# A list scheduler inside a kernel: operands that are also the result are counted, other durations in its cost table

## Chip, cores, metric

One core of a Trainium2 chip runs the whole program. The metric is the device time of one execution in microseconds; lower is better. Five engines have queues of their own: TensorE (PE, with its weight loads PEld), VectorE (DVE), ScalarE (ACT), GpSimd (POOL) and SyncE (SP), which issues the DMAs.

## What is computed

Two layers of a hybrid backbone on 640 tokens: 512 latent ones that are denoised and 128 context tokens, in float32, width 1024. Cut to what matters:

```python
def layer(x, cond):
    shift, scale, gate = split(silu(cond) @ w_mod + b_mod)
    h = rms_norm(x) * (1 + scale) + shift
    cols = split_cols(h @ w_in)             # q, k, v, gates for four mixers
    y = [neighbourhood_attention(cols), hgrn2(cols), mla(cols), window_attention(cols)]
    y = [o * silu(z) for o, z in zip(y, cols.z)]
    merged = sum(sigmoid(cols.g[b]) * (y[b] @ w_branch[b]) for b in range(4))
    return x + gate * (merged @ w_out)
x = layer(layer(x)); y = rms_norm(x)        # plus new keys, values and states as outputs
```

`hgrn2` is a gated linear recurrence in both directions, computed by chunks of 64 tokens; the decay between two tokens comes from the exponential of a difference of cumulated logarithms.

## The kernel before

All activations are held with features on the partitions and the 640 tokens along the free axis, in two halves of 320 columns. Each float32 matrix product is three matmuls of rounded parts: high times high, high times low, low times high. So each weight tile `wraw` (128x1024) is loaded by SyncE and split by two operations into `whi` (a copy) and `wlo` (a subtraction), and a projection half is 24 matmuls of 128x320 into a PSUM tile `pj_<name>`. Projections named `hq`, `hf`, `hb`, `ho`, `hz` belong to the recurrence, `ckv` and `qa` to latent attention (`mla`), `n..` to neighbourhood attention, `w..` to window attention, `g<branch><d>` to the merge gates; `pjm` is the product with `w_branch`, `pjo` that with `w_out`. Most working tiles have the name `slot`.

`hg_mix` is the recurrence. For each of eight levels it forms two tiles K and Q of decays (differences, then Exp, then products with keys and queries) and multiplies them on TensorE in 20 small products into `pslev`; VectorE or ScalarE copies these into place. Before that come Sigmoid and Ln on ScalarE, after it norms with Sqrt. Each change among these sets of functions is a table load on ScalarE. In the level loop, `K0, K1 = vw(K)` are views, and the products with the keys are

```python
                self.tt(K0, K0, kf0, ALU.mult)
                self.tt(K1, K1, kb1, ALU.mult)
```

so that the first input is the same object as the result. The attention parts (`probs`, `attend`, `pv_pair`) compute scores into `psS`, reduce them on VectorE into a column `nm`, take Exp on ScalarE, scale by the reciprocal `rc` of the sum, transpose on TensorE into `psT`, split, and multiply with the values into `psO`.

Nothing of this is issued as it is written. Every call is recorded as an operation by `Recorder.add`, with its predecessors; operations that may run on more than one engine are recorded with alternatives by `Recorder.alts` (`tt`, `ts`, `cpy`, `half`). `make_call` gives each alternative an engine time `step`, a time to the result `lat` and a flag `lock`. Then `Recorder.order` plays the program through in planned time: each engine that becomes free takes the ready operation of the lowest priority number; `take` gives an operation with alternatives to the engine that would end it first; an operation with `lock` waits until the last one with `lock` has ended, on VectorE or GpSimd; a table load costs 1290 ns more; TensorE's operations count double for a while after a long idle time. Slots and PSUM tiles are handed out as they come free in planned time. `emit` then issues each engine's operations in that order, and all instructions carry the line of `emit` (L561). `PLAN` is a hand-written interleaving of projections and mixing steps, `RANK` shifts whole kinds of steps, `AHEAD` and `WAHEAD` set how far the order may run ahead; the change touches none of them.

Of the kernel before, what the change touches and what calls it, by code (L numbers as in the profile page):

```python
# [22 lines left out]
P = 128  # L23
# [24 lines left out]
def f32(ap):  # L48
# [3 lines left out]

CAPS = {"slot": NSLOT, "w": NW, "ps": 8, "col": 32, "hhi": 1, "hlo": 1, "rstd": 4, "dec": 2, "fin": 2,
        "kr": 1}
SEM = 60
AHEAD = {"slot": (150, 6)}
EVICT = 230
WAHEAD, FIRST, MODP, EARLY = 150, 6, 0, 300
# [112 lines left out]
def nel(x):  # L171
    n = 1
    for s in x.shape[1:]:
        n *= s
    return n
# [19 lines left out]
OUT = ("out", "accum_out")  # L195
# [6 lines left out]
def make_call(eng, name, args, kw):  # L202
# [5 lines left out]
    out = kw["out"] if "out" in kw else args[0]  # L208
    ins = [x for x in refs if x is not out and x is not kw.get("accum_out")]
    n = max([nel(x) for x in refs], default=1)  # L210
    big = [x for x in ins if nel(x) > 1]
    psum = any(in_psum(x) for x in refs)
    if eng == "PE":
        lhs, rhs = (args[1], args[2])
        m, n = nel(lhs), nel(rhs)
        rows = lhs.shape[0]
        two = rhs.dtype == F32 and name == "matmul"
        c.tiled = (64 if rows <= 64 else 128, 64 if m <= 64 else 128)
        if c.tiled == (64, 64):
            step = 45  # L220
        elif two:
            step = max(2 * m / 1.15, 4 * n / 2.2, 120)
        else:
            step = max(m / 1.15, n / 2.18, 58)
        c.step, c.lat = step, step + 180
    elif eng == "DVE":
        two = len(big) >= 2 and not psum
        c.lock = two or (not psum and name in ("tensor_scalar", "tensor_copy") and n > 64)
        per, fix = 1.05, 150
        if name in ("tensor_scalar", "tensor_copy") and not psum:  # L230
            per = 0.6
        elif name == "tensor_tensor_scan":
            per = 2.1
        elif name == "tensor_tensor_reduce":
            fix = 250
        elif name == "reciprocal":
            per, fix = 6.0, 155
        elif name == "memset":
            per, fix = 0.8, 60
        t = fix + per * n  # L240
        c.step, c.lat = t - 80, t
    elif eng == "ACT":
        t = (170 if psum else 215) + 0.84 * n
        if "accum_out" in kw:
            t += 100
        c.step, c.lat = t - 95, t
        c.func = args[2].name if hasattr(args[2], "name") else str(args[2]).rsplit(".", 1)[-1]
    elif eng == "POOL":
        c.lock = True
        t = 60 + 0.8 * n if name == "memset" else 115 + 2.3 * n if len(big) >= 2 else 240 + 0.85 * n  # L250
        c.step, c.lat = t - 30, t
# [20 lines left out]
class Recorder:  # L272
# [81 lines left out]
    def order(self):  # L354
# [3 lines left out]
        n = len(ops)  # L358
# [13 lines left out]
        t = dict.fromkeys(ENGINES, 0.0)  # L372
# [43 lines left out]
        while len(out) < n:  # L416
# [54 lines left out]
                table = min(TABLES[c.func])  # L471
                step, lat = step + 1290, lat + 1290
            if e == "PE":
                if start - t[e] > 1400:
                    slow = start + 5000
                if start < slow:
                    step, lat = 2 * step, 2 * lat
            if c.tiled:
# [25 lines left out]
            for v in o.virts:  # L504
                v.left -= 1
                if v.left == 0 and v.cls != "static":
                    end = max(q.done for q in v.ops) + SEM
                    free[v.cls].append((end, v.real))
                    for x in ENGINES:
                        wake(x, end)  # L510
            for s in o.succs:
                s.npred -= 1
                same = s.alts[0].eng == c.eng and len(s.alts) == 1 and c.name != "dma_start"
                gap = 0 if same else SEM
                s.est = max(s.est, done + gap if s.preds[o] else start)
                if s.npred == 0:
                    enter(s)
# [1598 lines left out]
```

## Time and profile before

| what | us |
|---|---|
| median of 3 runs (lowest, highest) | 1517.21 (1515.16, 1521.85) |
| the profiled execution | 1516.75 |
| its span, first to last instruction | 1514.9 |
| TensorE busy | 1443.9 (95%) |
| VectorE busy | 1131.8 (75%) |
| ScalarE busy | 706.9 (47%) |
| GpSimd busy | 227.5 (15%) |

The span is what the rows below divide up; the execution's own time is 1.85 us longer. Busy time of an engine that waits for nothing costs nothing; a stretch is read by TensorE's idle time in it and by what that waited for. "pslev <-DVE slot" reads: an operation that writes `pslev` was held until VectorE had written a slot. Program lines are of no help here, since all have one, so rows are told apart by tile names and shapes.

### The profile page before, as it was taken

How to read it: one execution, taken by the hardware profiler on the slowest of the kernel's cores; microseconds unless marked ns; L12 is line 12 of the kernel's file. 1: busy time of each engine (PE TensorE's matmuls, PEld its weight loads, DVE VectorE, ACT ScalarE, POOL GpSimd, SP SyncE). 2: the span in 40 equal slices, each digit the busy share in tenths (PEclk: the TensorE clock that was granted, in tenths of full speed). 3: DMA queues.
4: the chain of work that ended last, by engine and by line, in shares of the span. 5: the costliest groups of instructions: out<-in, count | busy, mean ns of one | idle time of the engine just before them, and what ended most of it. 6: DMA issues, size and time to landing. Idle time of an engine off the chain costs nothing.

```text
span 1514.9 us, 28413 instructions
## 1 busy us (share of the span) xinstructions
PE 1443.9 (95%) x11228; PEld 1398.9 (92%) x11228; DVE 1131.8 (75%) x2452; ACT 706.9 (47%) x1406; POOL 227.5 (15%) x225
## 2 busy tenths in 40 slices
PE   5899999999999999999999999999999998999997
PEld 3798999999999989999999989998999998999997
DVE  7898876767656888996669997777666567875656
ACT  7685643455344344432457754445543433342222
POOL 1242310021111111200002541001101101010000
PEclk9999999999999999999999999999999999999998
DMA  9232111123225233435332111101422333222422
GB/s 348 77 86 75 41 60 39 54 78 87 87 89 180 85 114 109 140 128 191 138 119 73 38 57 59 55 29 60 128 71 87 98 117 94 66 75 89 152 98 98
DMA packets 72301, 146.47 MB, mean 97 GB/s; under 512 B 16936, under 2 KB 31848, under 8 KB 72168
## 3 DMA queue, kind: packets, MB, share of 16 engines
q1 hardware_dynamic: 72168, 144.66, 29.3%
q8 instruction: 88, 1.44, 0.4%
q14 instruction: 45, 0.37, 0.1%
HBM read 135.55 MB, written 8.24 MB: 95 GB/s over the span
## 4 chain that ended last, share of the span: by engine, by line
PE 70%; DVE 17%; ACT 6%; DMA 3%; issue 2%; SPq 1%; POOL 0%; DVEq 0%; POOLq 0%; ACTq 0%
DVE slot L561 14%; PE pj_gw L561 7%; PE pj_gm L561 7%; PE pjo L561 7%; PE pjm L561 6%; PE pj_gh L561 6%; PE pj_gn L561 6%; ACT slot L561 4%; PE psO L561 3%; PE pj_tok L561 3%; PE psS L561 3%; PE psT L561 3%; PE pjg L561 2%; DMA slot<-rel 2%; PE pj_ho L561 2%
## 5 line engine op out<-in xcount | busy, mean ns | idle before, releaser
L561 DVE TENSOR_TENSOR slot<-slot 128x320 f32<-128x320 f32 (+12 forms) x372 | 269.7, 746 | 39.8 <-ACT slot L561 22.1
L561 ACT ACTIVATE slot<-slot 128x640 f32<-128x640 f32 (+12 forms) x289 | 168.3, 605 | 133.8 <-DVE slot L561 117.1
L561 POOL TENSOR_TENSOR slot<-slot 128x320 f32<-128x320 f32 (+11 forms) x123 | 141.1, 1161 | 550.7 <-DVE slot L561 262.7
L561 DVE TENSOR_TENSOR wlo<-wraw,whi 128x1024 fp32r<-128x1024 f32 (+1 forms) x153 | 192.6, 1263 | 30.5 <-PE pj_gw L561 19.3
L561 ACT ACTIVATE whi<-wraw 128x1024 fp32r<-128x1024 f32 (+2 forms) x126 | 131.4, 1047 | 65.9 <-PE pj_gw L561 18.5
L561 ACT ACTIVATE slot<-slot,nm 128x384 f32<-128x384 f32 (+3 forms) x120 | 76.8, 640 | 101.9 <-DVE nm L561 101.2
L561 PE MATMUL pjm<-slot,whi 128*128 128x320 f32 x512 | 117.7, 311 | 0.0
L561 DVE SCALAR_TENSOR_TENSOR slot<-slot,pjm 128x320 f32<-128x320 f32 x128 | 61.5, 484 | 70.6 <-PE pjm L561 53.4
L561 PE MATMUL pjo<-slot,whi 128*128 128x320 f32 (+2 forms) x512 | 112.0, 309 | 0.0
L561 PE MATMUL psO<-slot 128*64 128x128 f32 (+2 forms) x620 | 81.7, 255 | 5.7 <-DVE slot L561 5.1
L561 PEld LDWEIGHTS pjm<-slot,whi 128*128 128x128 f32 x512 | 86.2, 188 | 0.0
L561 PEld LDWEIGHTS pjo<-slot,whi 128*128 128x128 f32 x512 | 85.4, 188 | 0.0
L561 PE MATMUL psS<-slot 96*128 96x320 f32 (+4 forms) x504 | 82.0, 289 | 0.7 <-DVE slot L561 0.5
L561 PE MATMUL pj_gh<-hhi,whi 128*128 128x320 f32 x256 | 81.7, 319 | 0.0
L561 PE MATMUL pj_gn<-hhi,whi 128*128 128x320 f32 x256 | 80.8, 316 | 0.3 <-ACT slot L561 0.3
L561 PE MATMUL pj_gm<-hhi,whi 128*128 128x320 f32 x256 | 81.1, 317 | 0.0
L561 PE MATMUL pj_gn<-hhi,wlo 128*128 128x320 f32 x256 | 79.8, 314 | 1.0 <-DVE wlo L561 1.0
L561 PE MATMUL pj_gm<-hlo,whi 128*128 128x320 f32 x256 | 80.7, 315 | 0.0
L561 PE MATMUL pj_gh<-hlo,whi 128*128 128x320 f32 x256 | 80.7, 315 | 0.0
L561 PE MATMUL pj_gh<-hhi,wlo 128*128 128x320 f32 x256 | 80.6, 315 | 0.0
L561 PE MATMUL pjo<-slot,wlo 128*128 128x320 f32 (+2 forms) x256 | 79.1, 311 | 1.4 <-DVE wlo L561 1.4
L561 PE MATMUL pjm<-slot,wlo 128*128 128x320 f32 x256 | 78.8, 311 | 1.5 <-DVE wlo L561 1.5
(316 smaller groups left out, 4276.0 us busy)
## 6 DMA issues: line engine op xcount, KB each, us to landing
wraw<-w_in SPq DMA_DIRECT2D x118, 512.0 KB
slot<-wmT SPq DMA_DIRECT2D x64, 256.0 KB
wraw<-w_out SPq DMA_DIRECT2D x26, 512.0 KB
slot<-wm SPq DMA_DIRECT2D x32, 256.0 KB
wraw<-w_br SPq DMA_DIRECT2D x16, 512.0 KB
slot<-xT SPq DMA_DIRECT2D x16, 320.0 KB
slot<-rel SPq DMA_DIRECT2D x32, 128.0 KB
xscr<-slot SPq DMA_DIRECT2D x16, 160.0 KB
```

What stands on the lines that cost most here:

```text
L561: getattr(eng[c.eng], c.name)(*[resolve(x) for x in c.args], **{k: resolve(x) for k, x in c.kw.items()})
```

## The change

It is in `make_call` and `Recorder.order` alone, and all of it is what the planner believes of durations:

- `big`, the list of inputs with more than one element, was taken from the operands that are not the same object as the result. Now it is taken from all arguments behind the result. For an operation like `tt(K0, K0, kf0)` or the in-place bias step of `na_bias`, two inputs count instead of one; so `lock` is set for it, and on GpSimd it costs 115 + 2.3 n ns instead of 240 + 0.85 n.
- On VectorE: plain copies and scalings 0.55 instead of 0.6 ns a column; `tensor_tensor_reduce` 165 (PSUM) or 205 instead of 250 ns; `scalar_tensor_tensor` 210 instead of 150 ns, but for 320 columns out of PSUM; one- and two-column scalings 208 ns.
- On ScalarE: 205 instead of 215 ns out of SBUF, 75 ns more for one or two columns and for 128 or 192 columns on all partitions, 265 ns for up to 10 columns out of PSUM.
- The delay from an operation to a dependent one on another engine was 60 ns (`SEM`) and is now 45 ns where the dependent one is on VectorE or ScalarE.
- TensorE counts as slow after 1200 ns of idle time instead of 1400, for 3200 ns instead of 5000.

```diff
--- before.py
+++ after.py
@@ -52,7 +52,7 @@
 
 CAPS = {"slot": NSLOT, "w": NW, "ps": 8, "col": 32, "hhi": 1, "hlo": 1, "rstd": 4, "dec": 2, "fin": 2,
         "kr": 1}
-SEM = 60
+SEM = {"PE": 60, "DVE": 45, "ACT": 45, "POOL": 60, "SP": 60}
 AHEAD = {"slot": (150, 6)}
 EVICT = 230
 WAHEAD, FIRST, MODP, EARLY = 150, 6, 0, 300
@@ -208,7 +208,8 @@
     out = kw["out"] if "out" in kw else args[0]
     ins = [x for x in refs if x is not out and x is not kw.get("accum_out")]
     n = max([nel(x) for x in refs], default=1)
-    big = [x for x in ins if nel(x) > 1]
+    big = [x for x in list(args[0 if "out" in kw else 1:]) + [v for k, v in kw.items() if k not in OUT]
+           if isinstance(x, Ref) and nel(x) > 1]
     psum = any(in_psum(x) for x in refs)
     if eng == "PE":
         lhs, rhs = (args[1], args[2])
@@ -228,11 +229,15 @@
         c.lock = two or (not psum and name in ("tensor_scalar", "tensor_copy") and n > 64)
         per, fix = 1.05, 150
         if name in ("tensor_scalar", "tensor_copy") and not psum:
-            per = 0.6
+            per = 0.55
         elif name == "tensor_tensor_scan":
             per = 2.1
         elif name == "tensor_tensor_reduce":
-            fix = 250
+            fix = 165 if psum else 205
+        elif name == "scalar_tensor_tensor":
+            fix = 150 if psum and n == 320 else 210
+        elif name == "tensor_scalar" and n <= 2:
+            fix = 208
         elif name == "reciprocal":
             per, fix = 6.0, 155
         elif name == "memset":
@@ -240,7 +245,11 @@
         t = fix + per * n
         c.step, c.lat = t - 80, t
     elif eng == "ACT":
-        t = (170 if psum else 215) + 0.84 * n
+        t = (170 if psum else 205) + 0.84 * n
+        if psum and n <= 10:
+            t = 265
+        elif not psum and (n <= 2 or (n in (128, 192) and out.p1 - out.p0 == P)):
+            t += 75
         if "accum_out" in kw:
             t += 100
         c.step, c.lat = t - 95, t
@@ -471,8 +480,8 @@
                 table = min(TABLES[c.func])
                 step, lat = step + 1290, lat + 1290
             if e == "PE":
-                if start - t[e] > 1400:
-                    slow = start + 5000
+                if start - t[e] > 1200:
+                    slow = start + 3200
                 if start < slow:
                     step, lat = 2 * step, 2 * lat
             if c.tiled:
@@ -504,14 +513,14 @@
             for v in o.virts:
                 v.left -= 1
                 if v.left == 0 and v.cls != "static":
-                    end = max(q.done for q in v.ops) + SEM
+                    end = max(q.done for q in v.ops) + 60
                     free[v.cls].append((end, v.real))
                     for x in ENGINES:
                         wake(x, end)
             for s in o.succs:
                 s.npred -= 1
                 same = s.alts[0].eng == c.eng and len(s.alts) == 1 and c.name != "dma_start"
-                gap = 0 if same else SEM
+                gap = 0 if same else SEM[s.alts[0].eng]
                 s.est = max(s.est, done + gap if s.preds[o] else start)
                 if s.npred == 0:
                     enter(s)
```

The order that comes out differs on each engine. In all, two-operand work of 320 columns on slots goes from 66 to 48 operations on GpSimd and from 116 to 134 on VectorE, and ScalarE's table loads from 47 to 54. Three places:

GpSimd, the levels of the first `hg_mix` of the first layer; a row is one operation, the numbers are partitions and the shape of 320 columns, by which the level is told (10x32 is the first). Before:

```order
L561 TENSOR_SCALAR whi<-wraw 128x864
L561 TENSOR_TENSOR wlo<-wraw,whi 128x864
L561 TENSOR_TENSOR slot<-slot 128x20x16
L561 TENSOR_TENSOR slot<-slot 128x10x32
L561 TENSOR_TENSOR slot<-slot 128x20x16 x3
L561 TENSOR_TENSOR slot<-slot 128x40x8 x2
L561 TENSOR_TENSOR slot<-slot 128x80x4
L561 TENSOR_TENSOR slot<-slot 128x160x2 x2
L561 TENSOR_TENSOR slot<-slot 128x5x64 x2
```

After:

```order
L570 TENSOR_SCALAR whi<-wraw 128x864 x2
L570 TENSOR_TENSOR slot<-slot 128x10x32 x2
L570 TENSOR_TENSOR slot<-slot 128x20x16 x2
L570 TENSOR_TENSOR slot<-slot 128x40x8
L570 TENSOR_TENSOR slot<-slot 128x160x2 x3
L570 TENSOR_TENSOR wlo<-wraw,whi 128x1024
```

Products of the levels have left GpSimd for VectorE, and a split of weights has come in between.

TensorE, the same stretch: where two groups of level products stand among the matmuls of `pj_hb` (a projection of the recurrence, halves told apart by the number). Before:

```order
L561 MATMUL pj_hb_1303<-hhi,whi 128x320
L561 MATMUL pslev<-slot 64x64 x20
L561 MATMUL pj_hb_1303<-hlo,whi 128x320
L561 MATMUL pj_hb_1303<-hhi,wlo 128x320
L561 MATMUL pslev<-slot 64x64 x20
```

After, around the first of the two groups:

```order
L570 MATMUL pslev<-slot 64x64 x80
L570 MATMUL pj_hb_1270<-hhi,whi 128x320
L570 MATMUL pj_hb_1270<-hlo,whi 128x320
L570 MATMUL pj_hb_1270<-hhi,wlo 128x320
L570 MATMUL pj_hb_1270<-hhi,whi 128x320
```

Three more matmuls of `pj_hb` follow, then 20 level products, then 25 matmuls, then the next 20 level products; before, only two matmuls stood between the two groups, and 100 level products stood ahead of them in place of 80.

ScalarE, the end of that `hg_mix`, beside the projection `pj_qa`. Before:

```order
L561 ACT_TABLE_LOAD
L561 ACTIVATE slot<-slot 128x640 x4
L561 ACTIVATE slot<-pj_ckv 128x320
L561 ACTIVATE slot<-slot 128x640
L561 ACT_TABLE_LOAD
L561 ACTIVATE slot<-slot 128x640 x2
L561 ACTIVATE slot<-pj_qa_1574 128x320
```

After:

```order
L570 ACT_TABLE_LOAD
L570 ACTIVATE slot<-slot 128x640 x2
L570 ACT_TABLE_LOAD
L570 ACTIVATE slot<-slot 128x640
L570 ACTIVATE slot<-pj_qa_1604 128x320
L570 ACTIVATE slot<-slot 128x640
L570 ACT_TABLE_LOAD
L570 ACTIVATE slot<-slot 128x640
```

Logarithms and exponentials now alternate there, with a table load at each turn.

## Rows read from the trace of the kernel before

**Rows 1.** The page, its parts 1 and 4: busy time; chain by engine.

```profile
PE 1443.9 (95%) x11228; PEld 1398.9 (92%) x11228; DVE 1131.8 (75%) x2452; ACT 706.9 (47%) x1406; POOL 227.5 (15%) x225
PE 70%; DVE 17%; ACT 6%; DMA 3%; issue 2%; SPq 1%; POOL 0%; DVEq 0%; POOLq 0%; ACTq 0%
```

**Rows 2.** Stretch; busy us: PE, PEld, DVE, ACT, POOL; clock, DMA, GB/s.

```profile
60.00:1480.00 1420.00, 1379.58 (x10823) 1348.27 (x10822) 1059.38 (x2282) 659.39 (x1322) 216.79 (x209) 1.00 0.28 90
60.00:165.00 105.00, 99.44 (x947) 95.78 (x947) 93.90 (x165) 73.10 (x121) 36.88 (x34) 0.98 0.23 67
480.00:600.00 120.00, 114.93 (x787) 112.51 (x786) 105.59 (x259) 48.55 (x109) 17.93 (x10) 0.99 0.40 132
800.00:890.00 90.00, 85.52 (x863) 82.76 (x862) 84.09 (x137) 68.03 (x101) 39.98 (x36) 1.00 0.20 63
1210.00:1330.00 120.00, 115.40 (x799) 112.41 (x798) 82.89 (x187) 45.57 (x98) 9.12 (x4) 1.00 0.30 95
```

**Rows 3.** The chain, shares by line: 86 to 165 us, then 800 to 890 us.

```profile
by line: DVE slot L561 26.4%; ACT slot L561 17.1%; ACT L561 11.4%; PE pj_hz L561 9.1%; PE pj_ho L561 8.9%; PE pshg L561 6.0%; issue 5.4%; DMA wraw<-w_in 4.6%; PE pj_hq L561 4.2%; DVE wlo L561 2.2%; PE psn L561 2.0%; DVE dec L561 1.4%; DVE w
...
by line: DVE slot L561 44.4%; PE pj_qa L561 8.0%; PE pj_ckv L561 7.8%; DVE wlo L561 5.8%; PE pjg L561 5.7%; ACT slot L561 5.3%; PE pj_hb L561 4.4%; issue 4.3%; ACT L561 4.3%; PE pj_ho L561 2.9%; PE pslev L561 2.6%; DVE dec L561 2.1%; PE pj_
```

**Rows 4.** Timeline of TensorE: start, length, what, count [idle time before, its releaser].

```profile
101.56 1.39 PE L561 MATMUL pslev<-slot 64*64 64x64 f32 x52 [1.02 <-issue]
...
107.68 1.21 PE L561 MATMUL pslev<-slot 64*64 64x64 f32 x40 [0.81 <-DVE slot L561]
...
835.09 1.21 PE L561 MATMUL pslev<-slot 64*64 64x64 f32 x40 [1.23 <-DVE slot L561]
...
839.43 1.21 PE L561 MATMUL pslev<-slot 64*64 64x64 f32 x40 [0.46 <-DVE slot L561]
...
841.24 1.21 PE L561 MATMUL pslev<-slot 64*64 64x64 f32 x40 [0.60 <-DVE slot L561]
```

**Rows 5.** GpSimd by form: count, busy us, mean ns, idle before and releasers.

```profile
L561 POOL TENSOR_TENSOR slot<-slot 128x320 f32<-128x320 f32 x66 | 65.2, 1006 | 151.4 <-ACT slot L561 73.4 <-DVE slot L561 73.2 <-PE pj_tok L561 4.6
L561 POOL TENSOR_TENSOR wlo<-wraw,whi 128x1024 fp32r<-128x1024 f32 x17 | 42.4, 2496 | 205.8 <-PE pjm L561 46.6 <-PE pj_gn L561 46.5 <-PE pjo L561 27.9
```

**Rows 6.** VectorE by form, the same columns.

```profile
L561 DVE TENSOR_TENSOR wlo<-wraw,whi 128x1024 fp32r<-128x1024 f32 x147 | 185.8, 1266 | 30.2 <-PE pj_gw L561 19.3 <-PE pjo L561 6.6 <-PE pj_wq L561 2.2
...
L561 DVE TENSOR_TENSOR slot<-slot 128x320 f32<-128x320 f32 x116 | 68.2, 613 | 9.6 <-ACT slot L561 8.9
...
L561 DVE CUSTOM_DVE_ANT_0 slot<-psS,slot 128x384 f32<-128x384 f32 x32 | 17.4, 552 | 16.2 <-PE psS L561 16.2
...
L561 DVE TENSOR_TENSOR slot<-psk,slot 64x320 fp32r<-64x320 f32 x16 | 7.8, 486 | 1.3 <-PE psu L561 1.1
```

**Rows 7.** Timelines of VectorE and GpSimd at 862 us.

```profile
862.33 3.05 DVE L561 TENSOR_TENSOR wlo<-wraw,whi 128x1024 fp32r<-128x1024 f32 x1
...
861.87 2.43 POOL L561 TENSOR_TENSOR wlo<-wraw,whi 128x1024 fp32r<-128x1024 f32 x1 [2.06 <-ACT whi L561]
```

**Rows 8.** ScalarE table loads, whole span, then 86 to 165 us; its timeline at 97 us.

```profile
L561 ACT ACT_TABLE_LOAD x47 | 60.3, 1283 | 4.6 <-DVE lbe L561 2.0 <-PE pjg L561 0.8 <-PEq L2112 0.7
...
L561 ACT ACT_TABLE_LOAD x9 | 11.5, 1283 | 0.1
...
96.90 0.77 ACT L561 ACTIVATE slot<-pj_hf 128x320 f32<-128x320 f32 x2
97.69 1.28 ACT L561 ACT_TABLE_LOAD   x1
98.98 0.74 ACT L561 ACTIVATE slot<-slot 128x640 f32<-128x640 f32 x1
```

**Rows 9.** TensorE waits: us in total, times, longest us.

```profile
PE psO L561 <- DVE slot L561: 5.1, 4, 2.1
...
PE pj_qa L561 <- DVE wlo L561: 2.1, 1, 2.1
...
PE psT L561 <- POOL slot L561: 1.9, 2, 0.9
```

## Prediction

> **What bounds the kernel now.** I read the page's first part and its chain first. TensorE is busy for 1443.9 us of 1514.9, and 70% of the chain that ended last is TensorE, 17% VectorE, 6% ScalarE; GpSimd has none of it [rows 1]. So time can only come out of the 71 us in which TensorE is idle, or go into new idle time. Then I split the span [rows 2]: between 60 and 1480 us TensorE is idle for 1420 - 1379.6 = 40.4 us; the other 31 us lie in the first 60 and the last 35 us, where loading and the final norm rule. The stretches to look at are the two in which the recurrent branch is mixed: 5.6 us idle in 60 to 165 us (first layer) and 4.5 us in 800 to 890 us (second layer), 10.0 us together; and 5.1 us and 4.6 us in the two stretches around the window attention, at 480 and 1210 us. In 800 to 890 us VectorE is busy for 84.1 of 90 us, in 60 to 165 us for 93.9 of 105. TensorE's clock is granted at 0.98 or more in all these rows, so it is almost always at the upper level, and I give the clock no term.
>
> Where the chain runs in these stretches [rows 3]: in 86 to 165 us VectorE's work on slots holds 26.4%, ScalarE's 17.1%, and a ScalarE row without a tile, the table loads, 11.4%. In 800 to 890 us VectorE's slots hold 44.4% and table loads 4.3%. TensorE's own holes are seen in its timeline [rows 4]: bursts of `pslev` that wait 1.02 and 0.81 us in the first layer, 1.23, 0.46 and 0.60 us in the second, 4.1 us in all.
>
> **The change, part by part.** The code computes the same. What changes is a table of durations inside the list scheduler, and by that the order, and the engine of those operations that have a choice. No instruction of TensorE or SyncE is added; only the sequence differs.
>
> *Operands that are also the result.* In `hg_mix` 48 products of 320 columns are written `tt(K0, K0, kf0)`. Before, one input was not counted, so the planner held GpSimd's time at 240 + 0.85 x 320 = 512 ns and took them for free of the lock between VectorE and GpSimd. The trace has 1006 ns for GpSimd's 128x320 form [rows 5]. Now the planner holds 115 + 2.3 x 320 = 851 ns and the lock. Counted in the two orders, GpSimd's two-operand work of this size falls from 66 to 48 and VectorE's rises from 116 to 134. So 18 leave GpSimd (18 x 1.006 = 18.1 us, none on the chain) and 18 come to VectorE (18 x 0.613 = 11.0 us) [rows 5, 6]. Against that, VectorE is held up less. A GpSimd operation and a VectorE operation of two SBUF operands exclude each other: at 862.33 us a `wlo` took 3.05 us that has a mean of 1.27 us, and it ended 1.08 us after GpSimd's `wlo` had ended at 864.30 us [rows 6, 7]. The mean of VectorE's 128x320 form, 613 ns, is 127 ns over the 486 ns of the form out of PSUM, which has no such partner [rows 6]; 116 x 0.127 = 14.7 us of holding up. If 18 of 66 causes go, 4.0 us go. VectorE's net is 11.0 - 4.0 = +7.0 us. By the mean of the two shares of the chain (0.26 and 0.44) 2.5 us of that lengthen the chain. How much of a microsecond on the chain reaches TensorE I take from the same stretches: in the first, 9.0 us of table loads lie on the chain (below) and TensorE is idle for 5.6 us, 2.1 of them for a `wlo` [rows 2, 9]; (5.6 - 2.1) / 9.0 is 0.4 at the most: **+1.0 us**. Bounds: -4.0 (only the holding up goes) and +7.0 (all on the path).
>
> *Table loads.* The order of before has 47 table loads, the new one 54: 27 instead of 22 up to the gates of the first layer, 27 instead of 25 after. They sit where Ln, Exp and Sigmoid alternate in `hg_mix` and its norms. 7 x 1.283 = 9.0 us of ScalarE [rows 8]. ScalarE is idle for 32 of the 105 us in the first stretch [rows 2], so they can hide; but 11.4% of 79 us are 9.0 us, that is 7 of the 9 loads there, so they mostly don't hide from the chain [rows 3, 8]. They hide from TensorE behind projections: a projection half has 24 matmuls and the planner pulls it forward. I take a quarter: **+2.2 us**, bounds 0 and +9.0. The Trainium skill (ScalarE: Activation LUTs, What ACT_TABLE_LOAD costs) puts 1283 ns for a load and some 1380 ns for a drain, 2.66 us for every switch. This trace agrees with the load and not with the drain: the load at 97.69 us starts 0.02 us after the eviction ended at 97.67 us, and the next operation starts 0.01 us behind it [rows 8]. By the page 7 switches would be 18.6 us and the quarter +4.7 us, an estimate, and the sum 1517.4 us.
>
> *Level products on TensorE.* In the first layer `pslev` bursts stood 2 matmuls apart, now 25; in the second they also stand further apart. The holes of [rows 4] are these places: TensorE went back to `pslev` before the level was ready. With other matmuls between them they close, unless the filler is missing later. **-3.0 us** of 4.1; bounds -4.1 and 0.
>
> *Softmax and evictions.* The reduction out of PSUM was held at 250 + 1.05 x 384 = 653 ns and is now 568; the trace has 552 [rows 6]. So the new number is nearer, and such numbers move where a transposition or a value product stands among the gate matmuls. At most places where TensorE waits for a softmax it is the same order as before: five matmuls of `pj_gm`, then eight of `psO`, with the wait of up to 2.1 us for VectorE [rows 9]. These stay. The two waits for GpSimd's scaling before `psT`, 1.9 us [rows 9], lie in `mla_pair`; there the scaling now goes to ScalarE: **-1.0 us**, bounds -1.9 and 0. Around the window attention the order changes most; the bound is half of the idle time there, 9.7 / 2 = 4.8 us either way, and I take **-1.0 us**, because the reductions' cost came nearer to its row.
>
> *Weights of `pj_qa`.* TensorE waited 2.1 us for a `wlo` by VectorE [rows 9]. It is GpSimd's now, where the form takes 2.50 us instead of 1.27 [rows 5, 6], but behind two fewer products. **0**, bounds -2.1 and +1.2.
>
> *Semaphore delay 45 instead of 60 ns for VectorE and ScalarE, the limit of 1200 ns for an idle TensorE, the plain copies and the 1024 and 640 forms:* all shift planned times by less than an instruction; no row of a wait hangs on them. 0.
>
> Sum: +1.0 + 2.2 - 3.0 - 1.0 - 1.0 + 0 = -1.8 us. The profiled execution took 1516.75 us, with 1514.9 of span, and it lies 0.46 us under the median of the three runs, which I leave alone. 1516.75 - 1.8 = **1515.0 us**. All low bounds together are -4.1 + 0 - 4.0 - 1.9 - 4.8 - 2.1 = -16.9 us, all high ones +9.0 + 7.0 + 4.8 + 1.2 = +22.0 us.
>
> **The rivals.** *ScalarE and VectorE take over the mixing stretches (slower).* Speaking for it: 7 of 9 loads lie on the chain, VectorE is busy for 93% of 800 to 890 us and gets more. Against: GpSimd gets out of its way. Price: the loads at 7 of 9, 7.0 us, and VectorE's 2.5 us of chain all become idle time of TensorE, and the spaced `pslev` bursts gain nothing as their inputs come later: +9.5 us, 1526.3 us. It decides as soon as the projections between two bursts are used up before the level is ready; TensorE's idle time in 60 to 165 us would then go from 5.6 to over 10 us.
>
> *The planner, nearer to the chip, closes holes everywhere (faster).* For it: the cost of the in-place products and of the reductions lies nearer to the rows. Against: most waits for softmax keep their order. Price: half of the 10.0 us of the mixing stretches, half of the 9.7 us at the window attention, and the 1.9 us before `psT`: -11.8 us, 1505.0 us.
>
> *It doesn't do what it says:* the corrected costs move operations between engines with slack, and new holes open where old ones close. TensorE's order is the same in most gate, output and attention stretches; 1516.8 us.
>
> **How the numbers follow.** Forecast 0.30, no effect 0.21: both lie within 0.5% of 1516.75 us (7.6 us either way, about what a measurement of this kernel can tell from no change), so same is 0.51, and the likeliest case's own range is 1509 to 1524 us. Faster 0.26, slower 0.23. The range reaches from a little under the faster rival, 1502, to a little over the slower one, 1528; the remaining fifth is for bounds that meet on one side.
>
> **What would show it.** After: 54 table loads of 1.28 us; GpSimd's busy time 18 to 35 us lower than 227.5, VectorE's up by about 7 to 11 us from 1131.8; `pslev` waits for VectorE under 2 us in all; TensorE's idle time in the two mixing stretches within 3 us of 10.0; the waits of `psO` and `psn` where they were. Wrong would be: a TensorE idle time in the mixing stretches over 18 us (the slower rival), or under 30 us between 60 and 1480 us in all (the faster one), or a new wait of several microseconds for a DMA, on which this sum has no term.

## The result and the profile after

| | before | after |
|---|---|---|
| median of the runs (lowest, highest), us | 1517.40 (1515.16, 1521.85) | 1552.62 (1550.98, 1556.23) |
| span of the profiled execution, us | 1514.9 | 1554.3 |
| mean granted clock of TensorE in it | 0.992 | 0.979 |

The changed kernel is slower: ratio 1.0232, 95% interval 1.0202 to 1.0262. The forecast was 1515.0 us and its range ended at 1528. Further down, each measured time is followed by its ratio to the kernel before, which ran beside it, and by the 95% interval of that ratio.

The page of the changed kernel, busy time and the chain by engine, as in [rows 1]:

```profile
PE 1471.5 (95%) x11228; PEld 1415.6 (91%) x11228; DVE 1125.1 (72%) x2466; ACT 722.8 (47%) x1426; POOL 194.2 (12%) x198
PE 68%; DVE 19%; ACT 5%; DMA 4%; issue 2%; SPq 1%; POOL 0%; DVEq 0%; ACTq 0%; POOLq 0%
```

TensorE's 11228 matmuls are the same. Yet its busy time rose by 27.6 us, and its idle time (span less busy) from 71.0 to 82.8 us, by 11.8; together 39.4 us, the difference of the spans. The stretches of [rows 2], the later ones moved along with the work; after the length come PE, PEld, DVE, ACT and POOL busy, the granted clock, DMA share and GB/s:

```profile
60.00:1480.00 1420.00, 1367.29 (x10618) 1326.13 (x10617) 1036.87 (x2285) 666.64 (x1329) 187.70 (x186) 0.98 0.27 87
60.00:165.00 105.00, 100.90 (x942) 95.94 (x941) 90.43 (x177) 79.95 (x125) 30.04 (x31) 0.97 0.23 67
822.00:917.00 95.00, 88.79 (x863) 85.84 (x862) 78.67 (x145) 67.84 (x102) 24.36 (x20) 0.96 0.19 60
500.00:625.00 125.00, 115.91 (x762) 113.20 (x762) 104.03 (x270) 47.88 (x107) 16.40 (x10) 0.95 0.34 107
1245.00:1370.00 125.00, 118.34 (x809) 114.92 (x807) 84.98 (x190) 45.35 (x96) 9.91 (x5) 0.99 0.29 92
```

All of the new idle time lies between 60 and 1480 us (52.7 us, it was 40.4). The two mixing stretches are idle for 4.1 and 6.2 us, 10.3 together, where it was 10.0: not there. Idle rose at the window attention of the first layer, from 5.1 to 9.1 us, and at that of the second, from 4.6 to 6.7; half of the new idle time is thus outside these four stretches, 3.4 us of it between 917 and 1245 us. And the clock column, 0.98 to 1.00 everywhere in [rows 2], now has 0.95, 0.96 and 0.97.

What that clock is worth stands in the hole at 525 us. TensorE's timeline there (start, length, what, [idle time before, its releaser]):

```profile
525.50 0.31 PE L570 MATMUL pj_gn<-hlo,whi 128*128 128x320 f32 x1
525.65 0.31 PE L570 MATMUL pjm<-slot,whi 128*128 128x320 f32 x1
527.85 0.41 PE L570 MATMUL pjm<-slot,whi 128*128 128x320 f32 x1 [1.89 <-ACT slot L570]
529.68 0.64 PE L570 MATMUL pj_wk<-hhi,wlo 128*128 128x320 f32 x1 [1.42 <-DVE wlo L570]
530.11 0.47 PE L570 MATMUL pj_wk<-hhi,whi 128*128 128x320 f32 x1
530.38 0.47 PE L570 MATMUL pj_wk<-hlo,whi 128*128 128x320 f32 x1
```

and the same place cut into windows, columns as above:

```profile
525.30:529.00 3.70, 1.07 (x6) 0.58 (x4) 3.60 (x7) 2.12 (x3) 0.00 (x0) 1.00 0.50 144
529.00:535.80 6.80, 6.12 (x23) 6.12 (x24) 6.59 (x15) 0.73 (x1) 0.00 (x0) 0.50 0.15 37
535.80:540.00 4.20, 4.20 (x31) 4.20 (x30) 4.17 (x7) 2.88 (x5) 0.00 (x0) 1.00 0.00 0
```

Two gaps of 1.89 and 1.42 us; from within the second one on, 6.8 us at 0.50, the lower level (1.2 GHz). Matmuls of 320 columns follow each other at 0.15 us ahead of the gaps and at 0.27 us behind them (0.147 and 0.267 in the median over both traces), so one microsecond at the lower level loses 1 - 0.147/0.267 = 0.45 us. The Trainium skill (TensorE: Matmul & The Clock Gate, Terms) prices such time at one half; these rows say 0.45. Over the span the time at the lower level is 2 x (1 - mean clock) x span: 24 us before, 65 us after. 41 us x 0.45 = 18 us. So of the 39.4 us, 11.8 are idle time, about 18 are the lower clock, and some 9 us of busy time are left.

The two traces show where these lie, if one counts from the start of each matmul to the start of the next, against the median of the same shape at the same level of the clock. The difference is then about 16 us for the lower level, 14 us at the idle gaps, and 9 us at spacings that are longer than their median although no idle time is counted there; 6 of these 9 us stand at `psT`, `pshg`, `psm` and `psn`. A matmul of 320 columns counts as busy for 0.31 us while the next one can start after 0.15, so a short wait is hidden in busy time.

### The profile page after: what moved, and what is told of

Read it like the earlier page. It is cut to its first block, busy times and chain, and to the rows that moved or that the text cites. A ratio compares the mean times of both kernels' runs of the same rounds, so it can differ in the third digit from the quotient of the medians.

```text
span 1554.3 us, 28415 instructions
## 1 busy us (share of the span) xinstructions
PE 1471.5 (95%) x11228; PEld 1415.6 (91%) x11228; DVE 1125.1 (72%) x2466; ACT 722.8 (47%) x1426; POOL 194.2 (12%) x198
## 4 chain that ended last, share of the span: by engine, by line
PE 68%; DVE 19%; ACT 5%; DMA 4%; issue 2%; SPq 1%; POOL 0%; DVEq 0%; ACTq 0%; POOLq 0%
DVE slot L570 15%; PE pj_gw L570 7%; PE pjo L570 7%; PE pj_gm L570 7%; PE pj_gn L570 6%; PE pj_gh L570 5%; PE pjm L570 5%; ACT slot L570 4%; PE psO L570 3%; PE psT L570 3%; PE psS L570 2%; PE pj_tok L570 2%; PE pjg L570 2%; DMA slot<-rel 2%; PE pj_nz L570 2%
## 5 line engine op out<-in xcount | busy, mean ns | idle before, releaser
L570 DVE TENSOR_TENSOR slot<-slot 128x320 f32<-128x320 f32 (+11 forms) x401 | 282.3, 727 | 52.8 <-ACT slot L570 26.8
L570 ACT ACTIVATE slot<-slot 128x640 f32<-128x640 f32 (+13 forms) x299 | 174.8, 602 | 142.7 <-DVE slot L570 124.8
L570 DVE TENSOR_TENSOR wlo<-wraw,whi 128x1024 fp32r<-128x1024 f32 (+2 forms) x152 | 187.3, 1237 | 38.5 <-PE pj_gw L570 23.3
L570 POOL TENSOR_TENSOR slot<-slot 128x320 f32<-128x320 f32 (+11 forms) x94 | 105.1, 1132 | 442.0 <-DVE slot L570 288.0
L570 PEld LDWEIGHTS pjo<-slot,whi 128*128 128x128 f32 x512 | 85.3, 188 | 0.8 <-ACT whi L570 0.8
L570 PEld LDWEIGHTS psS<-slot 128*128 128x128 f32 (+1 forms) x504 | 75.9, 192 | 6.8 <-ACT slot L570 6.4
L570 PE MATMUL psT<-ident,slot 128*128 128x128 f32 x392 | 65.4, 288 | 17.0 <-ACT slot L570 10.0
L570 PE MATMUL pj_gm<-hhi,wlo 128*128 128x320 f32 x256 | 81.2, 317 | 0.0
L570 DVE TENSOR_TENSOR slot<-psT,slot 128x512 fp32r<-128x512 f32 (+3 forms) x132 | 67.3, 546 | 18.1 <-ACT slot L570 14.8
```

Of the source, the lines that this page charges most:

```text
L570: getattr(eng[c.eng], c.name)(*[resolve(x) for x in c.args], **{k: resolve(x) for k, x in c.kw.items()})
```

## The first batch: parts of the change, and an edit that means nothing

Theory A was: one part of the change brings the loss. Theory B: any edit of the planner's numbers draws another order, and the kernel before is a favourable one.

**Operand counting alone.**

```diff
-    big = [x for x in ins if nel(x) > 1]
+    big = [x for x in list(args[0 if "out" in kw else 1:]) + [v for k, v in kw.items() if k not in OUT]
+           if isinstance(x, Ref) and nel(x) > 1]
```

> Of the change only the counting of operands that are also the result. It moves the 48 in-place products and the bias steps. If correct costs help by themselves: 1505 to 1513 us, with fewer than 66 operations of 128x320 on GpSimd. If the slower rival of the prediction holds (VectorE takes over the mixing stretches): 1524 to 1530 us, the loss in 60 to 165 and 800 to 890 us. Theory B: 1510 to 1550, the loss anywhere.

Measured: 1513.20 us, 0.995 (0.992 to 0.998). The part with which the prediction spent most words is a small gain.

**VectorE's durations alone.**

```diff
-            per = 0.6
+            per = 0.55
-            fix = 250
+            fix = 165 if psum else 205
+        elif name == "scalar_tensor_tensor":
+            fix = 150 if psum and n == 320 else 210
+        elif name == "tensor_scalar" and n <= 2:
+            fix = 208
```

> Of the change only the VectorE durations (copies 0.55 ns a column, reductions 165 or 205, scalar_tensor_tensor 210, short scalings 208), all else as before. Theory A, one part carries the loss, and it is the one that moved most numbers: 1545 to 1556 us, with the same hole around 525 to 555 us. Theory B, the greedy schedule jumps at any edit, so parts don't add: anywhere from 1510 to 1550 us, with holes at other places than in the changed kernel.

Measured: 1537.59 us, 1.0106 (1.0061 to 1.0152).

**ScalarE's durations alone.**

```diff
-        t = (170 if psum else 215) + 0.84 * n
+        t = (170 if psum else 205) + 0.84 * n
+        if psum and n <= 10:
+            t = 265
+        elif not psum and (n <= 2 or (n in (128, 192) and out.p1 - out.p0 == P)):
+            t += 75
```

> Of the change only the ScalarE durations (205 instead of 215, 75 ns more for one or two and 128 or 192 columns, 265 out of PSUM for up to 10). Theory A (VectorE's part carries the loss): within 8 us of 1517. Theory B: anywhere from 1510 to 1550 us; I expect some 1530, since the softmax order moves.

Measured: 1536.52 us, 1.0099 (1.0069 to 1.0129).

**One nanosecond.** The kernel before, with VectorE's fixed time in the planner at 151.

```diff
-        per, fix = 1.05, 150
+        per, fix = 1.05, 151
```

> The kernel before with one number altered by one nanosecond: the fixed part of every VectorE operation is held at 151 instead of 150 ns. Neither is nearer to the trace in any way that matters. Theory A (what counts is how right the durations are): 1517 us within 5 us. Theory B (the greedy schedule jumps at any edit): off by 10 to 35 us, and the planner's own planned end says later, so more likely 1530 to 1550 us.

Measured: 1537.00 us, 1.0118 (1.0094 to 1.0142). An edit without meaning costs as much as either table of durations. So 1% for a single part says nothing about that part, and theory A can't be read from such runs.

## The second batch: the hole at 525 us, and whether the planner's own end tells the time

The hole has a chain that the prediction had no term for. The chain of waits of the changed kernel, 515 to 531 us (start, length, what):

```profile
517.87 0.43 ACT slot L570
...
518.31 0.61 SPq L570
...
519.59 0.59 SPq L570
...
520.23 3.23 DMA slot<-slot
```

and VectorE's timeline there:

```profile
523.54 2.02 DVE L570 TENSOR_TENSOR slot<-slot 128x512 f32<-128x512 f32 x3 [5.27 <-DMA slot<-slot]
...
528.40 1.22 DVE L570 TENSOR_TENSOR wlo<-wraw,whi 128x1024 fp32r<-128x1024 f32 x1
```

ScalarE copies a query projection out of PSUM; SyncE issues the transfers that swap its halves for the rope (the rotary position embedding), 0.6 us apiece; the last lands 3.23 us after its issue; the rope work stands next in VectorE's queue and waits 5.27 us; the split of the `wk` weights stands behind it, and TensorE waits for that split. The planner reckons 110 ns for such an issue and 2 us from it to the landing.

**Two moves by hand** in the changed kernel's order, after planning. The numbers are positions of operations in the program.

```diff
+MOVES = [((4964, 4965, 4966, 4967, 4968, 4969, 4970), 5053), ((5226,), 5297)]
+        out = self.moved(out)
         self.out = out
```

> The changed kernel with two hand moves after planning, nothing else: the seven operations of one rope block (VectorE and one ScalarE) that stood at 523.54 us, where VectorE waited 5.27 us for its half-swap transfers, go behind the split of the wk weights that stood queued behind them (528.40 us) and behind a PSUM eviction; and the split of a gn0 weight that ended at 554.25 us goes into VectorE's wait before 544.05 us. Theory A (the hole at 525.6 to 529.7 us, 3.7 us of idle TensorE, and the 2.4 us before 554.25 us come from work queued in order behind operations that wait for a transfer, and the half-clock stretches at 529.0 and 552.9 us, 6.8 us each, are their sequel): TensorE's stretch 480 to 600 us loses its waits for the wk and gn0 splits, one or both half-clock stretches go, and the whole is 6 to 12 us shorter than the 1552.6 us of the changed kernel: 1541 to 1547. Theory B (the holes only uncover other waits, and what is won is lost again by the end): 1550 to 1556, with as much half-clock time as before the move.

Measured: 1553.66 us, 1.0237 (1.0202 to 1.0272), the changed kernel's time. TensorE's waits in 480 to 600 us (us in total, times, longest), first of the changed kernel:

```profile
PE psS L570 <- ACT slot L570: 2.9, 2, 2.1
PE pj_gn L570 <- DVE wlo L570: 2.2, 1, 2.2
PE pjm L570 <- ACT slot L570: 1.9, 1, 1.9
PE pj_wk L570 <- DVE wlo L570: 1.4, 1, 1.4
```

and with the two moves:

```profile
PE pj_wv L580 <- DVE wlo L580: 5.4, 1, 5.4
PE psS L580 <- ACT slot L580: 1.6, 2, 1.4
PE psT L580 <- DVE slot L580: 1.3, 1, 1.3
PE pj_wk L580 <- DVE wlo L580: 0.3, 1, 0.3
```

The wait for the split of `gn0` (a merge gate) went and that for `wk` fell from 1.4 to 0.3 us, as theory A said; the next split in the queue, that of `wv`, now stands behind the next rope block and costs 5.4 us. Theory B holds for this hole: mending one place uncovers the next, and the mean clock is 0.981, hardly above the 0.979 of the changed kernel.

**SyncE's issue at 600 ns** in the changed planner.

```diff
-        c.step, c.lat = (110, size / DMA_RATE) if eng == "SP" else (920, 1.8 * size / DMA_RATE)
+        c.step, c.lat = (600, size / DMA_RATE) if eng == "SP" else (920, 1.8 * size / DMA_RATE)
```

> The changed kernel with one more number: the planner charges SyncE 600 ns for each transfer that it issues in place of 110 (the chain of waits of the changed kernel shows 0.6 us from issue to issue ahead of the late rope block at 523.5 us). Theory A (the planner starts rope blocks before their half swaps can have landed, and work queues behind them): VectorE's wait for the half swaps (17.3 us in 5 in the changed kernel, the longest 5.3) falls to under 8 us and the time by 5 to 12 us, to 1541 to 1548. Theory B (a new order drawn, the wait moves elsewhere): 1515 to 1556, and TensorE's half-clock time need not fall.

Measured: 1543.77 us, 1.0164 (1.0127 to 1.0201). The time is in theory A's window, its reason is not. VectorE's waits for the half swaps, of the kernel before, of the changed kernel and of this one:

```profile
DVE slot L561 <- DMA slot<-slot: 11.7, 5, 4.0
```

```profile
DVE slot L570 <- DMA slot<-slot: 17.3, 5, 5.3
```

```profile
DVE slot L570 <- DMA slot<-slot: 15.5, 4, 7.2
```

15.5 us where under 8 was expected, and still more than the 11.7 of before: another order, not a cured wait.

**A table load at 1300 ns** in the planner of before.

```diff
-                step, lat = step + 1290, lat + 1290
+                step, lat = step + 1300, lat + 1300
```

> The kernel before with one number of the planner changed: an activation table load held at 1300 ns in place of 1290. No duration, wait or operation of the chip is changed by that; only the order jumps. By the planner's own reckoning (no measured time) the plan ends at 1479.7 us, where it reckons 1490.8 for the kernel before and 1502.6 for the changed one. Theory B (each order is a draw, spread over more than 1 per cent): anything from 1500 to 1540 us, and not the same as before. Theory C (the planner's own end tells an order's time, whatever edit gave it): 1480 + 25 to 28, 1502 to 1510 us, faster than both kernels.

Measured: 1523.33 us, 1.0033 (1.0009 to 1.0057). The planner reckoned 11 us less than for the kernel before; the chip took 5 us more. Theory C misses.

**Operand counting, and a matmul's latency 10 ns longer.**

```diff
-    big = [x for x in ins if nel(x) > 1]
+    big = [x for x in list(args[0 if "out" in kw else 1:]) + [v for k, v in kw.items() if k not in OUT]
-        c.step, c.lat = step, step + 180
+        c.step, c.lat = step, step + 190
```

> The kernel before with the in-place operands counted (that part of the change alone) and the planner's latency of a matmul 190 ns over its step in place of 180. The planner's own end of plan is 1479.4 us (1488.4 with the operand counting alone, which took 1513.2 us on the chip). Theory C (the planner's own end tells the time): 1502 to 1510 us. Theory B (each order is a draw): 1505 to 1540 us, no nearer to 1505 than to the other orders.

Measured: 1515.82 us, 0.9985 (0.9970 to 0.9999). Theory C misses again: 9 us less by its reckoning than counting alone, and no faster on the chip (0.9985 beside 0.995).

## The third batch: the clock by itself, and two more parts

**Gaps filled.** Same order as the changed kernel; ahead of 36 waiting matmuls, products with zeros.

```diff
+                if o.pos in FILL:
+                    into, k = FILL[o.pos]
+                    into = self.ops[into].eng.args[0]
+                    for _ in range(k):
+                        self.nc.tensor.matmul(resolve(into), ..., start=False, stop=False)
```

> The changed kernel, same order on every engine, with 249 products with zeros added on TensorE: ahead of 36 matmuls or transposes for which TensorE stood idle over 0.5 us in the changed kernel's trace, as many as fill that gap at 0.147 us each (2 to 18), accumulated into a group that is open anyway, so that nothing is added to a sum. The data that TensorE waits for comes no earlier. Theory D (half-clock stretches follow these gaps; the profiled span less half of the half-clock time less the idle time is the same, 1430 to 1438 us, in every order run so far, so each us at half clock costs half a us): the 68.3 us at half clock fall to 20 to 40 us and the time by 10 to 22 us, to 1531 to 1543. Theory E (the clock falls whatever is done in the gaps, or the fillers delay what is waited for): 1550 to 1565, with 60 us or more at half clock.

Measured: 1544.70 us, 1.0157 (1.0117 to 1.0197). Page and two rows of TensorE's timeline, the fillers in the hole of 525 us (here at 522):

```profile
PE 1486.8 (96%) x11477; PEld 1418.2 (92%) x11477; DVE 1126.8 (73%) x2466; ACT 722.5 (47%) x1426; POOL 193.9 (13%) x198
```

```profile
521.94 1.82 PE L572 MATMUL pj_wk<-zero,ident 128*128 128x320 bf16 x12
...
523.75 1.27 PE L572 MATMUL pj_wk<-zero,ident 128*128 128x320 bf16 x8
```

Its stretch from 60 to 1480 us:

```profile
60.00:1480.00 1420.00, 1391.08 (x10899) 1339.30 (x10898) 1043.28 (x2288) 668.90 (x1334) 187.32 (x186) 1.00 0.28 88
```

The clock there is 1.00 where the changed kernel has 0.98. Over the span it is 0.991; 2 x 0.009 x 1543.2 = 28 us at the lower level instead of 65. That is inside the 20 to 40 us of theory D, and 37 us x 0.45 = 17 us. The span fell by 11.1 us: 249 fillers of about 0.14 us are 34 us, and idle time fell by only 82.8 - 56.4 = 26.4, so the fillers overran their gaps by 8 us. The median fell by 7.9 us, 2 us short of theory D's window for that reason. Work that adds nothing to the result makes the kernel faster (1.0157 beside 1.0232, and the intervals don't overlap): the clock is shown as a cause. Its share, 17 us here and 16 to 18 above, is worked out and not measured by itself, since the fillers cost time too. And it is not the whole: with the time at the lower level back near that of before, and 8 us of overrun taken off, the kernel is still some 18 us slower than before.

**The same in the kernel with operand counting alone**, 161 products in 27 gaps.

```diff
+FILL = {135: (135, 9), 266: (266, 6), 260: (323, 11), ...}
```

> The kernel with only the in-place operands counted (1513.2 us), same order, with 161 products with zeros in 27 of its TensorE gaps, as in the run before this one. It had 29.9 us at half clock, 9.4 of them at the end, where no group is open. Theory D: 12 to 20 us at half clock, 1504 to 1510 us, faster than both kernels. Theory E: 1513 to 1520.

Measured: 1512.28 us, 0.9958 (0.9933 to 0.9982); counting alone was 0.995. Time at the lower level went from 27 to 21 us, 2.7 us by the 0.45, about what the fillers overran: no gain left. Theory D's 1504 to 1510 us is missed because little was there to win. Both kernels beat before and after.

**The semaphore wait alone.**

```diff
-SEM = 60
+SEM = {"PE": 60, "DVE": 45, "ACT": 45, "POOL": 60, "SP": 60}
-                gap = 0 if same else SEM
+                gap = 0 if same else SEM[s.alts[0].eng]
```

> The kernel before with the semaphore wait into VectorE and ScalarE at 45 ns in place of 60, and nothing else of the change. Theory B (every edit of a number draws another order, and the parts do not add up to the whole): another order within 1505 to 1540 us. Theory C (by the planner's own end, 1487.9 where it reckons 1490.8 for the kernel before and 1502.6 for the changed one): 1511 to 1518.

Measured: 1543.05 us, 1.0150 (1.0093 to 1.0208). Theory C falls for good: the planner's own end was 3 us better than for the kernel before, the chip is 24 us slower.

**The whole change without ScalarE's durations.**

```diff
-        t = (170 if psum else 205) + 0.84 * n
-        if psum and n <= 10:
-            t = 265
-        elif not psum and (n <= 2 or (n in (128, 192) and out.p1 - out.p0 == P)):
-            t += 75
+        t = (170 if psum else 215) + 0.84 * n
```

> The whole change without the ScalarE durations. If the ScalarE part (1.0099 by itself) added its share to the whole, this kernel would take 1552.6 less 15: 1536 to 1540 us. Theory B: anything from 1510 to 1555. Theory C (planner's own end 1499.5): 1530 to 1545. TensorE's idle plus half of its half-clock time tells the time in either case: the rest is 1430 to 1438 us.

Measured: 1544.62 us, 1.0158 (1.0117 to 1.0199): 8 us off the whole, where adding up would have it 15. The parts alone, 0.995, 1.0106, 1.0099 and 1.0150, would make 1.031 together, and the whole is 1.0232. That they don't add up is likely by both numbers but not shown by them: each ratio is known to 0.3 to 0.6%, and the difference is 0.8%. The fifth part, the limits for an idle TensorE, was never run alone.

## The fourth batch: the change, or the order that it drew

Three edits without meaning in the changed kernel, one in the kernel before. In this order: VectorE's fixed time 151, a table load 1300, a matmul's latency 190; and VectorE's fixed time 149 in the kernel before.

```diff
-        per, fix = 1.05, 150
+        per, fix = 1.05, 151
```

> The changed kernel with VectorE's fixed time at 151 ns in place of 150 in the planner, nothing else. Theory F (what the change put into the planner costs 2.3 per cent wherever its order lands): 1545 to 1560 us. Theory B (each order is a draw about 1 per cent above the kernel before; the changed kernel is one draw, at its upper end): 1520 to 1550, most likely near 1538, below the 1552.6 of the changed kernel.

Measured: 1550.96 us, 1.0202 (1.0129 to 1.0275).

```diff
-                step, lat = step + 1290, lat + 1290
+                step, lat = step + 1300, lat + 1300
```

> The changed kernel with an activation table load held at 1300 ns in place of 1290 in the planner. Theory F: 1545 to 1560 us. Theory B: 1520 to 1550.

Measured: 1549.69 us, 1.0193 (1.0123 to 1.0264).

```diff
-        c.step, c.lat = step, step + 180
+        c.step, c.lat = step, step + 190
```

> The changed kernel with a matmul's latency held 190 ns over its step in place of 180 in the planner. Theory F: 1545 to 1560 us. Theory B: 1520 to 1550.

Measured: 1542.34 us, 1.0145 (1.0079 to 1.0211).

```diff
-        per, fix = 1.05, 150
+        per, fix = 1.05, 149
```

> The kernel before with VectorE's fixed time at 149 ns in place of 150 in the planner, the counterpart of the run at 151 (1537.0 us). Theory B: 1505 to 1545 us, near 1535. If the order of the kernel before were an ordinary one among its neighbours, one of the two would have to lie below it: under 1517 us.

Measured: 1535.02 us, 1.0123 (1.0070 to 1.0176).

Neither theory holds alone. The changed kernel and its three neighbours lie at 1.0145 to 1.0232, mean 1.0193. The kernel before and its three neighbours (149, 151, table load 1300) lie at 1.0000 to 1.0123, mean 1.0069, with the kernel before itself the lowest. The medians of the two groups don't overlap, though the intervals of the nearest two (1.0145 and 1.0123) do. So, as an estimate from eight orders: about 0.7% of the loss is the favourable order of the kernel before, which all three edits of it gave up; about 1.2% belongs to what the change puts into the planner; 0.4% is the changed kernel's own draw. With a scatter of 0.4 to 0.6% in each group the 1.2% is uncertain by about 0.7. Operand counting and its neighbour (0.995 and 0.9985) lie below the group of before, so by these two orders the 1.2% is more likely to come from the durations, the semaphore wait or the limits for an idle TensorE, or from how they act together. Which of these, and why, is open: single orders can't tell it.

The spans, side by side, with TensorE's idle time and its time at the lower level (2 x (1 - clock) x span):

| kernel | span us | idle us | clock | lower level us |
|---|---|---|---|---|
| counting alone | 1511.0 | 66.9 | 0.991 | 27 |
| counting, latency 190 | 1513.3 | 66.4 | 0.989 | 33 |
| before | 1514.9 | 71.0 | 0.992 | 24 |
| before, table 1300 | 1523.6 | 72.9 | 0.988 | 37 |
| before, 151 ns | 1526.4 | 76.6 | 0.990 | 31 |
| before, 149 ns | 1531.8 | 81.1 | 0.987 | 40 |
| ScalarE's durations alone | 1534.1 | 74.9 | 0.984 | 49 |
| VectorE's durations alone | 1538.0 | 78.7 | 0.987 | 40 |
| semaphore wait alone | 1538.6 | 81.6 | 0.985 | 46 |
| changed, latency 190 | 1539.0 | 80.6 | 0.985 | 46 |
| changed, SyncE 600 ns | 1542.1 | 79.8 | 0.981 | 59 |
| changed without ScalarE's | 1543.6 | 79.2 | 0.983 | 52 |
| changed, 151 ns | 1546.6 | 85.3 | 0.984 | 49 |
| changed, two moves | 1548.9 | 83.4 | 0.981 | 59 |
| changed, table 1300 | 1550.1 | 80.3 | 0.978 | 68 |
| after | 1554.3 | 82.8 | 0.979 | 65 |

Span less idle less 0.45 of the last column is 1432 to 1442 us in all sixteen: whatever edit made the order, its time is told by these two columns within 10 us, where the spans differ by 43. What is left is not chance alone: it tends to rise with the span, from 1432 in the fastest order to 1442 in the slowest, the 9 us of longer spacings found above. The rows are one execution each; the run at 151 ns is the lowest of its eight (1528.14 us, median 1537.00).

## Why the prediction was wrong, step by step

**"I give the clock no term": the step that failed first.** It was read off 0.98 to 1.00 in [rows 2] and taken as a fact about the kernel; it is a fact about one order. Between 60 and 1480 us the trace of before has four stretches at the lower level, 14 us together; that of after has ten, 51 us, although TensorE's gaps of over 1 us there went only from 15 to 18. In place of the term of nothing the runs showed 16 to 18 of the 39 us.

**Orders as neutral, ±4.8 us: the second step that failed.** Without the clock the loss would still be some 21 us, in idle gaps and short waits. The bounds were half of the idle time that was there, which limits a gain, not a loss. In 500 to 625 us idle time rose by 4.0 us, inside that bound, but the clock in it fell from 0.99 to 0.95, and the same happened at places that the sum did not visit. That this order's neighbours are 0.3 to 1.2% slower could not be read in any row of before; only more orders show it.

**"A new wait of several microseconds for a DMA, on which this sum has no term"** was named as what would make it wrong, and came: 5.27 us at 523.54 us. It is not of a new kind, since VectorE already waited 11.7 us for half swaps before, up to 4.0 at a time, and the sum left that row out. But it is one of several holes; moving the work away from it gained nothing.

**Semaphore delay and the rest, "0".** The reason given, that the times shift by less than an instruction, is true and beside the point: 15 ns on that wait alone gave 1.0150, and 1 ns elsewhere 1.0118.

**Operands that are also the result, +1.0 us (-4.0 to +7.0).** The count was right, the sign of the sum wasn't. GpSimd, VectorE and ScalarE's table loads after (count, busy, mean ns, idle before and its releasers), beside [rows 5, 6, 8]:

```profile
L570 POOL TENSOR_TENSOR slot<-slot 128x320 f32<-128x320 f32 x48 | 48.0, 1021 | 138.2 <-DVE slot L570 84.2 <-ACT slot L570 39.9 <-ACT whi L570 11.6
```

```profile
L570 DVE TENSOR_TENSOR slot<-slot 128x320 f32<-128x320 f32 x134 | 71.7, 565 | 9.6 <-ACT slot L570 9.1
```

```profile
L570 ACT ACT_TABLE_LOAD x54 | 69.3, 1283 | 8.2 <-DVE slot L570 3.5 <-DVE lbe L570 2.5 <-PEq L2121 0.7
```

18 products moved, as counted. VectorE's mean fell from 613 to 565 ns, so the 18 cost it 3.5 us (71.7 less 68.2), not the 7.0 of the sum: 7.5 us of relief in place of 4.0. That fits less holding up by GpSimd's lock, but no run tested the lock by itself. All of VectorE is 6.7 us lower, where 7 to 11 more were forecast; GpSimd is 33.3 us lower, in the forecast's 18 to 35. Alone the step gave 0.995, about -7 us (-12 to -3 by the interval), where the sum had +1.0 and a bound of -4.0.

**Table loads, +2.2 us.** 54 loads of 1283 ns, as counted. With counting alone there are 52 of them in the trace and that kernel is faster than before with 47, which suggests that they hide well and cost nearer to 0 than to 2.2; no run has the loads alone.

**`pslev`, `psT`, `pj_qa`.** TensorE's waits before, beside [rows 4, 9], then after (us in total, times, longest):

```profile
PE psT L561 <- ACT slot L561: 6.4, 9, 1.4
...
PE pslev L561 <- DVE slot L561: 3.4, 5, 1.2
```

```profile
PE psT L570 <- ACT slot L570: 10.0, 8, 2.8
PE pslev L570 <- DVE slot L570: 6.0, 4, 2.3
...
PE psO L570 <- DVE slot L570: 2.1, 4, 0.8
...
PE psT L570 <- POOL slot L570: 1.7, 3, 0.8
```

`pslev` was to fall under 2 us (-3.0) and rose from 3.4 to 6.0: with matmuls between the bursts the level still came late, and the bursts met it in fewer, longer waits. (The 4.1 us of the sum held a wait of 1.02 us that ended by "issue", not by VectorE.) `psT` behind GpSimd was to lose 1.0 of 1.9 us and lost 0.2. `pj_qa` no longer waits: its lower bound, -2.1. `psO`, forecast to stay, fell from 5.1 to 2.1, and `psT` behind ScalarE, which was not in the sum, rose from 6.4 to 10.0.

**The rivals.** Slower by way of the mixing stretches (1526.3 us): its sign came, its mechanism didn't, since idle time there is 10.3 us and not 18. That these 10.3 us lie within 3 us of 10.0, as forecast, is luck: the first stretch fell from 5.6 to 4.1 us and the second rose from 4.5 to 6.2. The faster rival (1505.0 us) had neither its sign nor its idle time under 30 us; it is 52.7. "It doesn't do what it says" came nearest to what happened, new holes for old ones, but was priced at no change because holes were counted without the clock behind them.

## What to carry over

This list scheduler, with its greedy choices, turned every edit that was run, truer durations too, into a new order. So judge a change of its numbers against edits that mean nothing (here three of them cost 0.3 to 1.2%), and take several orders of each kind before a part is praised or blamed. Where TensorE is 95% busy, price its gaps twice: once as idle time and once as time at the lower clock that may follow, and write a term for the clock even where the profile of before shows almost none. Here 24 us at the lower level became 65.

## What the runs showed of the hardware

The clock does not answer to a gap's length alone. Behind 2.13 us of idle time at 1303 us the changed kernel stays at 1.00; around a gap of 1.21 us at 666.6 us the window's mean is 0.74. TensorE's timeline at the gaps, then the windows:

```profile
667.76 0.42 PE L570 MATMUL pjm<-slot,whi 128*128 128x320 f32 x1 [1.21 <-DVE slot L570]
...
1305.23 0.65 PE L570 MATMUL psS<-slot 128*128 128x256 f32 x4 [2.13 <-DVE slot L570]
```

```profile
1303.00:1308.00 5.00, 2.87 (x21) 2.80 (x21) 4.32 (x12) 1.11 (x4) 1.28 (x1) 1.00 0.34 118
...
666.00:672.20 6.20, 4.84 (x20) 4.17 (x21) 6.20 (x15) 1.80 (x2) 0.00 (x0) 0.74 0.55 201
```

Products with zeros raise the granted clock too: in the run with the gaps filled it is 1.00 between 60 and 1480 us, where the changed kernel has 0.98. And a half swap of 64 KB within SBUF for the rope took 3.23 us from the end of its issue to its landing. The Trainium skill (DMA: Bandwidth & Descriptors, Anatomy of one DMA — SWDGE (gpsimd) path) gives about 2 us of fixed cost, and the time of the bytes on top, for a transfer that GpSimd issues. This one was issued by SyncE and took longer; why is not shown here.
